# The memory's sum of squares behind the output projection, and memory values traced before a norm's element-wise part

## The chip, the core and the metric

One core of a Trainium2 chip runs the whole program in one launch. The metric is device time in microseconds. TensorE (PE) multiplies matrices and loads its weights (PEld) beside that; VectorE (DVE), ScalarE (ACT) and GpSimd (POOL) work element by element; SyncE (SP) issues most of the loads from memory. Each engine runs its own list of instructions in order, and waits on semaphores for the others.

## The reference

Two transformer blocks on 256 tokens of width 1024, everything in float32. The first: windowed and differential attention side by side, gated, merged, an output projection with a norm behind it, and a gated FFN (2816 wide), with a norm behind that. The second: a delta-rule mixer and a sparse latent attention, then cross-attention to a memory of 256 rows, then another FFN. What the change touches is the end of the first block and the memory's side of the cross-attention:

```python
# first block
merged = g_swa * (o_swa @ w_branch_swa[l]) + g_diff * (o_diff @ w_branch_diff[l])
h = h + rms_norm(merged @ w_out[l], post_mix_gain[l])
u = rms_norm(h, pre_ffn_gain[l])
...
# second block, cross-attention
mn = rmsnorm(mem, g_mem[l])
kvx = (mn @ w_xkv[l]).reshape(b, m_len, 2, X_HEADS, X_DH)
```

with `rmsnorm(x, g) = x * rsqrt(mean(x*x) + 1e-6) * g`. The memory does not depend on the tokens, so its keys and values can be computed at any time before the cross-attention.

## The kernel before

Tokens lie along the free axis: a tensor of 1024 features by 256 tokens is eight tiles of 128 x 256. A product is computed in halves for accuracy. ScalarE rounds a weight tile of 128 x 1024 to `wh` (L311; in a few places VectorE, L309), VectorE or GpSimd subtracts to get the rest `wl` (L313), and TensorE runs 24 matmuls for one output tile (`gemm`, L326): eight times `wh` with the activation's high and low half, then eight times `wl` with the high half. The raw tiles come by SyncE, three in flight; `wh` and `wl` have three buffers each.

The stages in question, in order:

- The branch projection `w_bs` (L813 to L823), eight groups. VectorE turns each result into a gated sum `mt` (L816, L817), ScalarE and VectorE split it into `m_h` and `m_l` (L287, L288). In the same loop `mem_split` (L776) works on the memory: VectorE makes its halves `mem_h` and `mem_l`, GpSimd squares its eight tiles and adds them up in `memt[:, 0]` (L781, L783).
- The memory's scale (L826 to L835): two matmuls with one column each (L388, one for 128 memory rows) sum the squares over the partitions; VectorE makes the rsqrt of the two columns by Newton steps (L377 to L381, L368 to L370), spreads it to two diagonals (L393), a matmul broadcasts it over the partitions (L833), and ScalarE copies that to `rsm` (L835). The result as a column, `rsm_t`, scales the memory's values.
- The output projection `w_out1` with `post_norm` (L837): eight groups; ScalarE keeps each result and its square, VectorE adds the squares (L401). Then the norm: a matmul with ones sums over the partitions (L351), `rsqrt_chain` (ScalarE's Ln and Exp, four steps on VectorE), eight products (L854) on VectorE, eight adds of the residual on GpSimd (L855), splits into `uh` and `ul` (L290, L291), squares again, and a second L351 with its rsqrt, whose scale is used only behind the FFN's products.
- `mem_keys` (L787): eight groups of the memory's keys; each result is multiplied by `rsm` on its way out of PSUM (L789).
- The first FFN, `ffn_in` (L871) and `w_fo1` with `post_norm` again (the norm before mixing), and behind it `mem_values` (L791), whose results are scaled by `rsm_t` (L806).

The order of the instructions on the engines is not the order of the code. A scheduler takes the program as traced, models its times, and builds each engine's list; a step traced earlier has precedence, and a tile of a pool has to be given back before the next with the same tag is used. The sums of both norms and of the memory and its broadcast are tiles `st` of the pool `ps_o`, tag `o`, one buffer:

```python
st = psum_pool.tile([P, 512], F32, name="st", tag="o")
pe.matmul(st[:, :n], ones, acc, start=True, stop=True)
```

So the order in which they are traced is the order in which they run.

Of the kernel before, what the change touches and what calls it, by code (L numbers as in the profile page):

```python
# [16 lines left out]
F32 = mybir.dt.float32  # L17
# [3 lines left out]
AF = mybir.ActivationFunctionType  # L21
# [4 lines left out]
P = 128  # L26
NT = 256
# [189 lines left out]
MEMG = 3  # L217
# [3 lines left out]
def _program(tc, d, out):  # L221
    nc = tc.nc
    ctx = ExitStack()
    pe, act, dve, pool, sp = nc.tensor, nc.scalar, nc.vector, nc.gpsimd, nc.sync
# [7 lines left out]
    with ctx:  # L232
# [12 lines left out]
        def carve(n, p=P):  # L245
            used[0] += n
            return base[:p, used[0] - n:used[0]]
# [8 lines left out]
        def G(n, j=0):  # L256
            o, w = _GC[n]
            return gcol[:, o + j:o + j + 1]
# [14 lines left out]
        ones_d = carve(P)  # L273
# [3 lines left out]
        ones_1 = carve(P)  # L277
# [70 lines left out]
        def rsqrt_of(psum_pool, acc, ones, n, out_t):  # L348

            st = psum_pool.tile([P, 512], F32, name="st", tag="o")  # L350
            pe.matmul(st[:, :n], ones, acc, start=True, stop=True)  # L351
            rsqrt_chain(st[:, :n], n, out_t)

        def rsqrt_chain(st, n, out_t, p=P):
            a = gpool.tile([P, NK], F32, name="rs_a", tag="rs_a", bufs=2)[:p, :n]
            b = gpool.tile([P, NK], F32, name="rs_b", tag="rs_b", bufs=1)[:p, :n]
            act.activation(a, st, AF.Ln, bias=eps[:p, :])
            act.activation(a, a, AF.Exp, scale=-0.5)
            dve.tensor_tensor(b, a, a, OP.mult)
            dve.scalar_tensor_tensor(b, st, EPS, b, OP.add, OP.mult)  # L360
            dve.tensor_scalar(b, b, -0.5, 1.5, OP.mult, OP.add)
            dve.tensor_tensor(out_t, b, a, OP.mult)

        def newton(y, h):

            t = gpool.tile([P, 16], F32, name="nt_t", tag="nt_t", bufs=2)[:, :y.shape[1]]
            for _ in range(3):
                dve.tensor_tensor(t, y, y, OP.mult)  # L368
                dve.tensor_tensor(t, t, h, OP.mult)
                dve.scalar_tensor_tensor(y, t, 1.5, y, OP.add, OP.mult)  # L370

        def rsqrt_tok(st, nb, add=EPS):

            m = gpool.tile([P, 16], F32, name="nt_m", tag="nt_m", bufs=2)[:, :nb]
            h = gpool.tile([P, 16], F32, name="nt_h", tag="nt_h", bufs=2)[:, :nb]
            y = gpool.tile([P, 16], F32, name="nt_y", tag="nt_y", bufs=2)[:, :nb]
            dve.tensor_scalar(m, st, add, None, OP.add)  # L377
            dve.tensor_scalar(h, st, -0.5, -0.5 * add, OP.mult, OP.add)
            yi = y.bitcast(I32)
            dve.tensor_scalar(yi, m.bitcast(I32), 1, None, OP.logical_shift_right)  # L380
            dve.tensor_scalar(yi, yi, -1.0, MAGIC, OP.mult, OP.add)  # L381
            newton(y, h)
            return y

        def sums_tok(dst, acc, col, nb):

            for b in range(nb):
                pe.matmul(dst[:, b:b + 1], acc[:, b * P:(b + 1) * P], col[:, 0:1], start=True, stop=True)  # L388

        def diag_tok(dg, y, nb, n):  # L390
            for b in range(nb):
                w = min(P, n - b * P)
                dve.tensor_scalar(dg[:, b * P:b * P + w], ident[:, :w], y[:, b:b + 1], None, OP.mult)  # L393
# [23 lines left out]
        opool = new_pool(b1, "ps_o", 1, PSUM)  # L417
# [5 lines left out]
        st = opool.tile([P, 512], F32, name="st", tag="o")  # L423
        for _ in range(WARM):
            tc.keep_in_program_order(pe.matmul(st[:, :P], one.to_broadcast([P, P]), one.to_broadcast([P, P]),
                                               start=True, stop=True))
# [10 lines left out]
        st = opool.tile([P, 512], F32, name="st", tag="o")  # L437
# [283 lines left out]
        qs, fill = [], list(range(16))  # L721
# [48 lines left out]
        mhp = new_pool(mhst, "memhl", side="right")  # L770
        mem_h = mhp.tile([P, 8, NT], F32R, name="mem_h")
        mem_l = mhp.tile([P, 8, NT], F32R, name="mem_l")
        memt = mhp.tile([P, KT, NT], F32, name="memt")
# [13 lines left out]
        def mem_keys():  # L787
            for j in range(8):
                gemm(d["w_xk"][j], mems, NT, lambda o, j=j: dve.tensor_tensor(kx[:, j, :], o, rsm, OP.mult))  # L789

        def mem_values(groups):  # L791
            for g in groups:
                ps = [mm.tile([P, 512], F32, name="mm", tag="mm") for _ in range(2)]
                for kh in range(2):
                    h, l = load_w(d["w_xv"][g][:, kh * 1024:(kh + 1) * 1024], KT)
                    for tb in range(2):
                        tok = slice(tb * P, (tb + 1) * P)
                        for k in range(4):
                            kk_ = 4 * kh + k
                            cols = slice(k * NT, (k + 1) * NT)  # L800
                            o = ps[tb][:, :NT]
                            pe.matmul(o, mem_h[:, kk_, tok], h[:, cols], start=(kk_ == 0), stop=False)
                            pe.matmul(o, mem_l[:, kk_, tok], h[:, cols], start=False, stop=False)
                            pe.matmul(o, mem_h[:, kk_, tok], l[:, cols], start=False, stop=(kk_ == 7))  # L804
                for tb in range(2):
                    dve.tensor_scalar(vx[:, tb, g * NT:(g + 1) * NT], ps[tb][:, :NT], rsm_t[:, tb:tb + 1], None,  # L806
                                      OP.mult)
# [15 lines left out]
            mem_split(j)  # L823

        tc.keep_in_program_order(act.preload_act_table_set(EXP_LN))
        st = opool.tile([P, 512], F32, name="st", tag="o")  # L826
        sums_tok(st, memt[:, 0, :], ones_d, 2)
        rsm_t = mhp.tile([P, 2], F32, name="rsm_t")
        dve.tensor_copy(rsm_t, rsqrt_tok(st[:, :2], 2))
        dg = mhp.tile([P, NT], F32, name="dgm")  # L830
        diag_tok(dg, rsm_t, 2, NT)
        st = opool.tile([P, 512], F32, name="st", tag="o")
        pe.matmul(st[:, :NT], ones_1, dg, start=True, stop=True)  # L833
        rsm = mhp.tile([P, NT], F32, name="rsm")
        act.activation(rsm, st[:, :NT], AF.Copy)  # L835

        def post_norm(src_w, xs, gain, res, res_out, g_next, whole=False):  # L837

            fg = mpool.tile([P, 8, NT], F32, name="fg", tag="fg")
            acc = gpool.tile([P, NK], F32, name="acc", tag="acc", bufs=1)[:, :NT]  # L840
            for j in range(8):
                def use(o, j=j):
                    act.activation(fg[:, j, :], o, AF.Copy, scale=G(gain, j))
                    sumsq(j, o, acc, NT)
                gemm_long(src_w[j], xs, NT, use)
            rr = gpool.tile([P, NK], F32, name="rs", tag="rs", bufs=2)
            rsqrt_of(opool, acc, ones_d, NT, rr[:, :NT])
            if whole:
                u = gpool.tile([P, KT, NK], F32, name="u", tag="uh")
            else:  # L850
                uh, ul = new_u()
            acc2 = gpool.tile([P, NK], F32, name="acc2", tag="acc2", bufs=1)[:, :NT]
            for j in range(8):
                dve.tensor_tensor(fg[:, j, :], fg[:, j, :], rr[:, :NT], OP.mult)  # L854
                pool.tensor_tensor(res_out[:, j, :], fg[:, j, :], res[:, j, :NT], OP.add)  # L855
                if whole:
                    act.activation(u[:, j, :NT], res_out[:, j, :], AF.Copy, scale=G(g_next, j))
                else:
                    split(uh[:, j, :NT], ul[:, j, :NT], res_out[:, j, :], G(g_next, j))
                sumsq(j, res_out[:, j, :], acc2, NT)  # L860
            rs2 = gpool.tile([P, NK], F32, name="rs", tag="rs", bufs=2)
            rsqrt_of(opool, acc2, ones_d, NT, rs2[:, :NT])
            if whole:
                return [u[:, k, :NT] for k in range(8)], rs2[:, :NT]
            return [(uh[:, k, :NT], ul[:, k, :NT]) for k in range(8)], rs2[:, :NT]

        h1 = rpool.tile([P, KT, NT], F32, name="h1", tag="resB")
# [3 lines left out]
        def ffn_in(pool_, src_w, us, rs, f_h, f_l):  # L871
            for j in range(FT):
# [7 lines left out]
                def use_u(o, sg=sg, j=j):  # L880
# [20 lines left out]
        relb = carve(8, 32)  # L901
        late(relb, d["rel_bias"])

        mem_keys()


# [16 lines left out]

        x1 = rpool.tile([P, KT, NK], F32, name="x1", tag="resA")[:, :, :NT]
        us, rs = post_norm(d["w_fo1"], [(f_h[:, k, :], f_l[:, k, :]) for k in range(FT)],
                           "post_ffn", h1, x1, "g_mix", whole=True)
        fst.close()


        mem_values(range(MEMG))  # L930

# [536 lines left out]
        for c in range(2):  # L1470
            gb = ppool.tile([P, 512], F32, name="s", tag="s")
            for h in range(4):
                pe.matmul(gb[:, h * P:(h + 1) * P], gg[:, 4 * c + h:4 * c + h + 1].to_broadcast([P, P]), triu,
                          start=True, stop=True)
# [88 lines left out]
        for h in range(4):  # L1563
# [28 lines left out]
            o = opool.tile([P, 512], F32, name="o", tag="o")  # L1592
            o = o.rearrange("p (a b) -> p a b", a=2)
# [105 lines left out]
```

## Time and profile before

| | |
|---|---|
| runs | 1011.46, 1011.47, 1014.0 us; median 1011.47 |
| the profiled execution | 1014.09 us, its span 1012.3 us |
| mean granted clock of TensorE | 0.984 of full speed |
| busy share of the span | TensorE 96%, weight loads 90%, VectorE 71%, ScalarE 54%, GpSimd 31% |
| branch projection | about 285 to 320 us |
| output projection | about 320 to 342 us |
| first norm and memory keys | about 342 to 380 us |
| norm before mixing, memory values | about 558 to 585 us |

The times of single instructions are counted from the start of the span. A row of the timeline merges equal instructions that follow each other: start, time from the first's start to the last's end, engine, line, what is written from what, and how many. Matmuls are pipelined, so a row's 0.28 us of one is longer than the 0.12 us from one start to the next. A releaser in brackets is what ended the engine's idle time just before.

### The profile page before, as it was taken

The numbers are of one execution on the slowest core, as the hardware profiler recorded it, in microseconds if no ns is written. First come the engines' busy times: TensorE is split into PE (matmuls) and PEld (weight loads), VectorE is DVE, ScalarE is ACT, GpSimd is POOL, SyncE is SP. The second block draws the span as 40 slices with busy tenths as digits, with TensorE's granted clock in tenths as the row PEclk, the third lists the DMA queues.
The fourth block names the chain that finished last, engine by engine and source line by source line (L and its number), as shares of the span: only waits on it lengthen the run. The fifth ranks groups of instructions, "written<-read, shape, count | busy, mean of one in ns | idle before, by whom it ended". The sixth has DMA issues, their size and how long they took to land. (4 is left out here: it accounts for less than half of the span.)

```text
span 1012.3 us, 18979 instructions
## 1 busy us (share of the span) xinstructions
PE 974.1 (96%) x7356; PEld 916.1 (90%) x7356; DVE 722.8 (71%) x1468; ACT 544.8 (54%) x1089; POOL 312.3 (31%) x294
## 2 busy tenths in 40 slices
PE   9889999999978999999999899999999999999996
PEld 8779999998978999999999788787799999999885
DVE  7998899887697696656455638977687676666444
ACT  4556677666544555555454444335666555555433
POOL 6865468655491032221100302221021002222002
PEclk9998999999997999999999899999999999999998
DMA  6333333333434555555666232333045255555552
GB/s 238 129 104 101 109 107 124 120 110 105 167 125 148 188 204 186 187 187 183 214 200 198 83 133 91 122 114 106 1 150 205 64 186 188 187 187 186 182 192 88
DMA packets 42026, 149.31 MB, mean 147 GB/s; under 512 B 4728, under 2 KB 5376, under 8 KB 41808
## 3 DMA queue, kind: packets, MB, share of 16 engines
q1 hardware_dynamic: 40896, 145.47, 42.6%
q0 software_dynamic: 608, 2.03, 0.7%
q8 instruction: 58, 0.95, 0.4%
q10 hardware_dynamic: 432, 0.59, 0.2%
q14 instruction: 32, 0.26, 0.1%
HBM read 147.01 MB, written 1.06 MB: 146 GB/s over the span
## 5 line engine op out<-in xcount | busy, mean ns | idle before, releaser
L311 ACT ACTIVATE wh<-raw 128x1024 fp32r<-128x1024 f32 (+1 forms) x244 | 256.2, 1052 | 222.7 <-PE mm L326 134.3
L313 DVE TENSOR_TENSOR wl<-raw,wh 128x1024 fp32r<-128x1024 f32 (+1 forms) x220 | 274.0, 1247 | 85.8 <-ACT wh L311 83.7
L326 PE MATMUL mm<-uh,wh 128*128 128x256 f32 (+1 forms) x1112 | 280.5, 287 | 1.3 <-DVE vbm L540 0.9
L326 PE MATMUL mm<-ul,wh 128*128 128x256 f32 (+1 forms) x1112 | 279.0, 286 | 0.2 <-DVE ul L291 0.2
L326 PEld LDWEIGHTS mm<-uh,wh 128*128 128x128 f32 x1112 | 211.1, 190 | 4.6 <-DVE vbm L540 1.1
L326 PEld LDWEIGHTS mm<-ul,wh 128*128 128x128 f32 x1112 | 211.5, 190 | 1.3 <-DVE ul L291 0.5
L326 PE MATMUL mm<-uh,wl 128*128 128x256 f32 (+1 forms) x1112 | 162.5, 285 | 0.0
L326 PEld LDWEIGHTS mm<-uh,wl 128*128 128x128 f32 x1112 | 145.2, 191 | 0.8 <-issue 0.3
L878 POOL TENSOR_TENSOR sg<-sg,rs 128x256 f32<-128x256 f32 x44 | 49.4, 1126 | 233.8 <-ACT sg L877 229.3
L313 POOL TENSOR_TENSOR wl<-raw,wh 128x1024 fp32r<-128x1024 f32 x30 | 72.4, 2414 | 51.9 <-ACT wh L311 51.9
L337 PE MATMUL mm<-u,raw 128*128 128x256 f32 x320 | 73.1, 382 | 0.2 <-DMA raw<-w_pr 0.2
L337 PEld LDWEIGHTS mm<-u,raw 128*128 128x128 f32 x320 | 59.5, 190 | 9.5 <-DVE y L995 0.6
L882 DVE TENSOR_TENSOR ft<-mm,sg 128x256 f32<-128x256 f32 x42 | 17.8, 424 | 52.0 <-PE mm L326 51.5
L326 PE MATMUL mm<-f_h,wh 128*128 128x256 f32 x176 | 41.1, 276 | 0.0
L326 PE MATMUL mm<-f_l,wh 128*128 128x256 f32 x176 | 41.1, 276 | 0.0
L876 DVE TENSOR_TENSOR sg<-mm,rs 128x256 f32<-128x256 f32 x40 | 17.0, 424 | 31.4 <-PE mm L326 31.3
L1633 PE MATMUL ac<-wh,f_h 128*128 128x512 f32 (+1 forms) x110 | 38.4, 349 | 0.0
L1636 PE MATMUL ac<-wh,f_l 128*128 128x512 f32 (+1 forms) x110 | 38.1, 347 | 0.0
L1637 PE MATMUL ac<-wl,f_h 128*128 128x512 f32 (+1 forms) x110 | 37.8, 347 | 0.0
L326 PEld LDWEIGHTS mm<-f_l,wh 128*128 128x128 f32 x176 | 33.0, 188 | 0.0
L326 PEld LDWEIGHTS mm<-f_h,wh 128*128 128x128 f32 x176 | 33.0, 188 | 0.0
L855 POOL TENSOR_TENSOR x<-fg,h 128x256 f32<-128x256 f32 x8 | 7.7, 997 | 66.6 <-PE mm L804 66.6
(544 smaller groups left out, 2205.8 us busy)
## 6 DMA issues: line engine op xcount, KB each, us to landing
raw<-w_gu SPq DMA_DIRECT2D x88, 512.0 KB, 4.3
raw<-w_dn SPq DMA_DIRECT2D x22, 512.0 KB, 3.7
raw<-w_pr SPq DMA_DIRECT2D x20, 512.0 KB, 3.6
raw<-w_gate SPq DMA_DIRECT2D x16, 512.0 KB, 3.6
raw<-w_out SPq DMA_DIRECT2D x16, 512.0 KB, 3.7
raw<-w_fo SPq DMA_DIRECT2D x16, 512.0 KB, 3.8
raw<-w_kb SPq DMA_DIRECT2D x8, 512.0 KB, 3.7
raw<-w_vb SPq DMA_DIRECT2D x8, 512.0 KB, 3.7
```

The lines of the kernel that those rows point to most:

```text
L311: act.activation(h[:, :kt * c], raw[:, :kt * c], AF.Copy)
L313: eng.tensor_tensor(l[:, :kt * c], raw[:, :kt * c], h[:, :kt * c].bitcast(F32), OP.subtract)
L326: pe.matmul(o, w[:, k * P:(k + 1) * P], xs[k][i], start=(first and n_ == 0), stop=(last and n_ == len(steps) - 1))
L337: pe.matmul(o, raw[:, k * P:(k + 1) * P], x, start=(k == 0), stop=(k == len(xs) - 1))
L855: pool.tensor_tensor(res_out[:, j, :], fg[:, j, :], res[:, j, :NT], OP.add)
L876: dve.tensor_tensor(sg, o, rs, OP.mult)
L878: pool.tensor_tensor(sg, sg, rs, OP.mult)
L882: dve.tensor_tensor(t, o, sg, OP.mult)
L1633: m = pe.matmul(o, f_h[:, k, tok], h[:, cols], start=(k == 0), stop=False)
L1636: pe.matmul(o, f_l[:, k, tok], h[:, cols], start=False, stop=False)
L1637: pe.matmul(o, f_h[:, k, tok], l[:, cols], start=False, stop=(k == FT - 1))
```

## The change

Two edits. The block that makes the memory's scale is traced behind the output projection's whole `post_norm`, just ahead of `mem_keys`, where it stood before the projection. And `post_norm` gets a parameter `fill`, a function that it calls between its first rsqrt and the element-wise part; the norm before mixing uses it to trace the first group of memory values there, and the other two follow behind it as before.

```diff
         tc.keep_in_program_order(act.preload_act_table_set(EXP_LN))
-        st = opool.tile([P, 512], F32, name="st", tag="o")
-        sums_tok(st, memt[:, 0, :], ones_d, 2)
-        rsm_t = mhp.tile([P, 2], F32, name="rsm_t")
-        dve.tensor_copy(rsm_t, rsqrt_tok(st[:, :2], 2))
-        dg = mhp.tile([P, NT], F32, name="dgm")
-        diag_tok(dg, rsm_t, 2, NT)
-        st = opool.tile([P, 512], F32, name="st", tag="o")
-        pe.matmul(st[:, :NT], ones_1, dg, start=True, stop=True)
-        rsm = mhp.tile([P, NT], F32, name="rsm")
-        act.activation(rsm, st[:, :NT], AF.Copy)
-
-        def post_norm(src_w, xs, gain, res, res_out, g_next, whole=False):
+        def post_norm(src_w, xs, gain, res, res_out, g_next, whole=False, fill=None):
...
             rsqrt_of(opool, acc, ones_d, NT, rr[:, :NT])
+            if fill is not None:
+                fill()
...
         late(relb, d["rel_bias"])
 
+        st = opool.tile([P, 512], F32, name="st", tag="o")
+        sums_tok(st, memt[:, 0, :], ones_d, 2)
...
+        rsm = mhp.tile([P, NT], F32, name="rsm")
+        act.activation(rsm, st[:, :NT], AF.Copy)
+
         mem_keys()
...
-                           "post_ffn", h1, x1, "g_mix", whole=True)
+                           "post_ffn", h1, x1, "g_mix", whole=True, fill=lambda: mem_values([0]))
         fst.close()
 
-        mem_values(range(MEMG))
+        mem_values(range(1, MEMG))
```

TensorE, in the branch projection; `os_h` and `os_l` are its activation halves, `memt` the squares of the memory. The row with a minus is the first of the two sums:

```order
 L326 MATMUL mm<-os_l,wh 128x256
 L326 MATMUL mm<-os_h,wl 128x256 x8
-L388 MATMUL st<-base,memt 128x1
 L326 MATMUL mm<-os_h,wh 128x256
 L326 MATMUL mm<-os_l,wh 128x256
```

What moved: the first sum stood between the fifth and the sixth group, the second (not shown) between the eighth and the first group of the output projection; both are gone from there.

TensorE, after the output projection, at the end of the second key group; `mem_h` and `mem_l` are the memory's halves, `acc` and `acc_4676` the sums of squares of the norm's first and second rsqrt:

```order
 L326 MATMUL mm<-mem_h,wh 128x256
 L351 MATMUL st<-acc,base 128x256
+L326 MATMUL mm<-mem_l,wh 128x256
+L326 MATMUL mm<-mem_h,wh 128x256
+L326 MATMUL mm<-mem_l,wh 128x256
+L326 MATMUL mm<-mem_h,wl 128x256 x8
+L351 MATMUL st<-acc_4676,base 128x256
+L388 MATMUL st<-base,memt 128x1 x2
+L902 MATMUL st<-dgm,base 128x256
+L326 MATMUL mm<-mem_h,wh 128x256
```

What moved: the second norm sum, the memory's two sums and its broadcast now stand right behind the second key group, and key groups 3 to 8 behind them. Before, the second norm sum stood inside the fourth FFN group.

VectorE, the same place, as it stands in the change (with the line numbers of the change; the other Newton steps and the copy to the column lie between the two pieces):

```order
L401 TENSOR_TENSOR acc_4676<-acc_4676,sq 128x256 x2
L1222 COPY small<-base 128x128
L1235 STREAM_SHUFFLE row<-small 128x16 x2
L359 TENSOR_TENSOR rs_b<-rs_a 128x256
L360 SCALAR_TENSOR_TENSOR rs_b<-st,rs_b 128x256
L361 TENSOR_SCALAR rs_b<-rs_b 128x256
L362 TENSOR_TENSOR rs<-rs_b,rs_a 128x256
L377 TENSOR_SCALAR nt_m<-st 128x2
...
L393 TENSOR_SCALAR dgm<-base,rsm_t 128x128 x2
L789 TENSOR_TENSOR kx<-mm,rsm 128x256 x3
```

What moved: the Newton steps stand behind the norm's last adds, a copy of a constant and the second rsqrt; they stood beside the end of the branch projection. The first three key evictions (L789) follow them in one piece; before, seven of the eight stood among the norm's steps. From the middle of the first FFN to the end of the program the lists of all engines are the same, but for the small matmul of the bias table (L916 before), which stood behind the fifth FFN group and now stands behind the last one, and the copy of its result.

## Rows read from the trace of the kernel before

**Rows 1.** Busy time, share of the span and instructions of each engine
```profile
PE 974.1 (96%) x7356; PEld 916.1 (90%) x7356; DVE 722.8 (71%) x1468; ACT 544.8 (54%) x1089; POOL 312.3 (31%) x294
```

**Rows 2.** What TensorE waited for, whole span: total us, times, longest
```profile
PE st L388 <- POOL memt L783: 7.9, 1, 7.9
PE mm L804 <- DVE wl L313: 5.0, 2, 4.4
```

**Rows 3.** TensorE in order of time: start, us, instruction, [idle before it <-releaser]
```profile
299.07 1.11 PE L326 MATMUL mm<-os_h,wl 128*128 128x256 f32 x8
...
308.07 0.59 PE L388 MATMUL st<-base,memt 128*128 128x1 f32 x2 [7.89 <-POOL memt L783]
```

**Rows 4.** Windows: length, busy of five engines, granted clock, DMA share, GB/s
```profile
303.00:304.00 1.00, 0.00 (x0) 0.00 (x0) 1.00 (x2) 0.00 (x0) 1.00 (x1) 0.82 0.00 0
...
313.00:314.00 1.00, 1.00 (x7) 1.00 (x7) 0.00 (x0) 0.73 (x2) 0.00 (x0) 0.56 0.00 0
314.00:315.00 1.00, 1.00 (x10) 1.00 (x10) 0.97 (x2) 0.00 (x0) 0.00 (x0) 1.00 0.00 0
```

**Rows 5.** VectorE in order of time, end of the branch projection
```profile
302.30 1.74 DVE L313 TENSOR_TENSOR wl<-raw,wh 128x1024 fp32r<-128x1024 f32 x1
...
310.03 0.41 DVE L288 TENSOR_TENSOR m_l<-mt,m_h 128x256 fp32r<-128x256 f32 x1
...
322.29 0.42 DVE L288 TENSOR_TENSOR m_l<-mt,m_h 128x256 fp32r<-128x256 f32 x1
```

**Rows 6.** Waits of all engines, 265 to 425 us
```profile
DVE mt L816 <- PE mm L326: 4.8, 3, 3.6
```

**Rows 7.** TensorE in order of time, output projection to first FFN groups
```profile
324.32 1.07 PE L326 MATMUL mm<-m_h,wl 128*128 128x256 f32 x8
...
346.42 0.59 PE L351 MATMUL st<-acc,base 128*128 128x256 f32 x2
...
347.20 1.12 PE L326 MATMUL mm<-mem_h,wl 128*128 128x256 f32 x8
...
373.20 0.28 PE L326 MATMUL s<-uh,wh 128*128 128x256 f32 x1
...
376.03 0.28 PE L326 MATMUL mm<-uh,wh 128*128 128x256 f32 x1
...
379.29 0.28 PE L326 MATMUL mm<-uh,wh 128*128 128x256 f32 x1
```

**Rows 8.** ScalarE in order of time, first rsqrt of the norm
```profile
347.05 0.47 ACT L357 ACTIVATE rs_a<-st,base 128x256 f32<-128x256 f32 x1 [1.90 <-PE st L351]
347.42 1.05 ACT L311 ACTIVATE wh<-raw 128x1024 fp32r<-128x1024 f32 x1
```

**Rows 9.** VectorE in order of time, the norm after the output projection
```profile
353.05 6.07 DVE L854 TENSOR_TENSOR fg<-fg,rs 128x256 f32<-128x256 f32 x8
...
360.73 1.35 DVE L291 SCALAR_TENSOR_TENSOR ul<-h,base,uh 128x256 fp32r<-128x256 f32 x2
...
363.81 1.26 DVE L291 SCALAR_TENSOR_TENSOR ul<-h,base,uh 128x256 fp32r<-128x256 f32 x3
...
378.51 0.42 DVE L359 TENSOR_TENSOR rs_b<-rs_a 128x256 f32<-128x256 f32 x1
```

**Rows 10.** GpSimd in order of time, the same norm
```profile
353.61 7.79 POOL L855 TENSOR_TENSOR h<-fg,hT 128x256 f32<-128x256 f32 x8 [45.60 <-DVE fg L854]
```

**Rows 11.** DMA issues, 260 to 400 us: count, KB, median us to landing
```profile
base<-const_b POOLq DMA_DIRECT2D x1, 384.0 KB, 5.7
```

**Rows 12.** VectorE in order of time, the memory's Newton steps
```profile
322.02 0.16 DVE L380 TENSOR_SCALAR nt_y<-nt_m 128x2 int32<-128x2 int32 x1
...
324.18 0.16 DVE L370 SCALAR_TENSOR_TENSOR nt_y<-nt_t,nt_y 128x2 f32<-128x2 f32 x1
```

**Rows 13.** TensorE in order of time, the norm before mixing
```profile
558.33 0.59 PE L351 MATMUL st<-acc,base 128*128 128x256 f32 x2
```

**Rows 14.** VectorE in order of time, the same norm
```profile
574.78 2.00 DVE L401 TENSOR_TENSOR acc<-acc,sq 128x256 f32<-128x256 f32 x4
```

More of the change, by code (lines that the diff above doesn't have):

```diff
@@ L902, in _program @@
         late(relb, d["rel_bias"])
+        st = opool.tile([P, 512], F32, name="st", tag="o")
+        sums_tok(st, memt[:, 0, :], ones_d, 2)
+        rsm_t = mhp.tile([P, 2], F32, name="rsm_t")
+        dve.tensor_copy(rsm_t, rsqrt_tok(st[:, :2], 2))
+        dg = mhp.tile([P, NT], F32, name="dgm")
+        diag_tok(dg, rsm_t, 2, NT)
+        st = opool.tile([P, 512], F32, name="st", tag="o")
+        pe.matmul(st[:, :NT], ones_1, dg, start=True, stop=True)
+        rsm = mhp.tile([P, NT], F32, name="rsm")
+        act.activation(rsm, st[:, :NT], AF.Copy)
         mem_keys()
```

## The prediction

> **What bounds the kernel now.** I read the busy line first: TensorE is busy 974.1 us of 1012.3, so 38 us of idle time are all that a reordering can win, and any new idle time there lengthens the run [rows 1]. Then the list of what TensorE waited for: the longest wait by far is 7.9 us, and it is the first of the two matmuls that this change moves, waiting for GpSimd's sum of squares of the memory [rows 2, 3]. [...] Last I read the engines in order of time through the branch projection, the output projection and the norm behind it, since there the order listing moves instructions.
>
> **Part 1: the wait that goes.** The wait ends at 308.07, and the matmuls then run at half clock until about 313.9, which costs half of 5.9 us, 2.9 us [rows 3, 4]. On paper 7.9 + 2.9 = 10.8 us come back. But VectorE runs without a gap up to the end of the fourth m_l subtraction (310.03 + 0.41 = 310.4), so nothing before that comes earlier [rows 5]. From there to the last m_l subtraction (ending 322.71) it spent 12.3 us, of which 4.8 were waits for the late TensorE [rows 5, 6], and 0.4 us were four small steps of the memory's rsqrt that now leave. So the last m_l is ready 5.2 us earlier, at 317.5. TensorE then has 18 matmuls of the first two output groups left, at 24 per 2.83 us (373.20 to 376.03) [rows 7]: done at 319.7. Before, the last eight of them started at 324.32 and took 0.95: 325.3 [rows 7]. I take a gain of 5.6 us. The ends are 10.8 (if VectorE's backlog hid nothing) and 2.7 (if the thin stretch around 312 to 317 us, where TensorE now waits piecemeal for m_h and m_l, brings the clock down once more, another 2.9).
>
> **Part 2: the wait that comes.** In the new order the memory's two sums and the broadcast of its scale stand behind the second key group *and* behind the norm's second sum (the L351 on the second accumulator). All these borrow one small PSUM pool, and the listing puts them in one file: norm sum, memory sums, broadcast, then key groups 3 to 8. Before, key groups 2 to 8 and the first FFN groups ran beside the norm's element-wise work. Now TensorE stands still from the end of key group 2 until the whole chain is through. Behind the waiting matmul are six key groups (17 us of work at 2.83) and all of the FFN; on ScalarE six weight casts stand behind the copy of the scale; on VectorE the key evictions stand behind the Newton steps. Key group 2 ends at 347.20 + 0.95 = 348.2 before, so at 342.6 now [rows 7]. From there, step by step:
> - VectorE still subtracts one weight tile, whose cast ends at 347.42 + 1.05 - 5.6 = 342.9 [rows 8]; with 1.2 us for it, 344.1.
> - The four steps of the first rsqrt at 0.42 each [rows 9]: 345.8.
> - The eight products, slowed by GpSimd's adds beside them, 6.07 us [rows 9]: 351.9.
> - Eight ul subtractions and seven adds of squares. Three run while GpSimd still adds, at 0.68; the others at about 0.4 [rows 9, 10]: between 6.3 and 7.0 us, I take 6.6: 358.5.
> - Norm sum to ScalarE's Ln 0.63 (346.42 to 347.05) [rows 7, 8], Ln and Exp 0.9: 360.0. VectorE also has a copy of a constant before its next step, which GpSimd's queue fetches only after its adds: 345.8 + 0.56 + 7.79 + 5.7 for the landing = 359.9 [rows 10, 11], then 0.4 for three small steps: 360.3. The two arrive together.
> - Two rsqrt steps, after which the bank is free, 0.85; the two memory sums about 0.6: 361.7.
> - Newton: 322.02 to 324.34 before, less one subtraction between (0.42), is 1.9 [rows 12]; two first steps, the copy and the two diagonals about 0.85 more: 364.5.
> - Broadcast and ScalarE's copy, again 0.63 + 0.4: 365.5; with the three small matmuls at half clock, 366.0.
>
> So TensorE idles 23.4 us, and key group 3 starts at 366.0 instead of 348.2: 17.8 us later, the 5.6 already taken off. As a check, the norm ahead of the mixing block has the same chain with memory values beside it: its first sum is at 558.33, its last add of squares ends at 576.8, 18.4 us [rows 13, 14]; mine is 340.8 to 358.5, 17.7 us.
>
> After so long an idle stretch the clock is at half, and I charge the 2.9 us of the stop at 300 to 314 us [rows 4]. Something comes back: between key group 3 and the end of the fourth FFN group TensorE needed 31.1 us (348.2 to 379.29) for ten groups that take 28.3 at 2.83, and 0.2 for the norm's sum; the remaining 2.6 us were waits for pieces of the norm that are long done now [rows 7]. Three key groups have their weights cast before the stop, so the casts behind the copy come in time, and SyncE's loads, three tiles ahead, wait with them at no cost.
>
> **Part 3: edits with no price.** The first memory values are traced ahead of the element-wise part of the norm before mixing. In the listing nothing moves there: TensorE, VectorE and ScalarE have the same order before and after, because the scheduler had put these values beside that norm already. The 4.4 us wait of that place, the greater part of the second row of [rows 2], therefore stays: 0 us. The matmul that makes the bias table moves behind the first FFN's last group: one small matmul at another place, and its two DMAs keep their place in GpSimd's queue behind the FFN's products: 0 us.
>
> **The sum.** +17.8 + 2.9 - 2.6 = +18.1 us. The profiled execution took 1014.1 us (span 1012.3), 2.6 above the median of the runs, 1011.5. Its sum is 1032.2; on the median it is 1029.6, and I predict **1030 us**. TensorE is the bound in all later stages, so nothing there takes the delay up.
>
> **The rivals.**
> - *The clock falls a second time* (0.14). In the thin stretch of part 1 TensorE has about 3.4 us of matmuls in 6.8 us. For it: the earlier fall came in a stretch of standing still. Against it: each of these gaps is under 2 us, where that fall came some 3 us into one unbroken wait [rows 4]. Price 2.9: 1033.
> - *A shorter chain* (0.14). Without weight subtractions and key evictions between them, VectorE's products and GpSimd's adds may run closer. At 0.42 a product the eight take 3.4 instead of 6.07, if GpSimd's 7.79 shrinks as well, and the constant lands earlier; two more us from the small steps. Price -5: 1025. Against it: the 6.07 and the 7.79 are of eight products and eight adds that ran back to back already [rows 9, 10].
> - *The queue does not hold* (0.02), the case on the other side. If matmuls of key groups 3 to 8 could pass the waiting sums, only part 1 would remain: 1011.5 - 5.6 = 1006. It decides from the point where a ready matmul starts before an older one that waits. Against it: at 304.04 the last weights of the next branch group were ready, and TensorE stood until 308.07 behind the one waiting sum [rows 3, 5], with no weight load either [rows 4].
>
> [...]
>
> - *The gaps cancel* (0.05). To come out even, key group 3 would have to start by 347.9, a gap of 5.3 us. GpSimd's adds alone take 7.79 [rows 10], so this needs the built order to matter less than listed, by some cover that I do not see.
>
> **How the numbers follow.** Forecast 0.65 (1026 to 1035), second fall of the clock 0.14, shorter chain 0.14, cancelling 0.05, passing 0.02. A difference under 0.3% (3 us) can't be told from none here. All but the last two are slower by more than that: slower 0.93; cancelling is spread over same and faster, 0.03 and 0.02; with passing, faster 0.04. The range takes in the second fall of the clock and most of the shorter chain: 1023 to 1036.
>
> **What would show it.** In the changed profile: no wait of TensorE for the memory's sums near 300 us and a full clock there; one gap of 20 to 24 us after the second key group, released by VectorE and ScalarE in three pieces (norm sum, memory sums, broadcast); half clock for some 6 us behind it; then no waits until the fourth FFN group. A wait of 4 to 5 us for memory values in the next norm, as before. I am wrong if that gap is under 10 us, if key matmuls run beside the norm's products, or if the branch projection still waits as long.

## The result and the profile after

The changed kernel took 1030.57 us (median of 4 runs, 1030.2 to 1031.01) against 1012.08 us of the kernel before (4 runs, 1011.46 to 1014.0): the ratio is 1.0181, with a 95% interval of 1.0169 to 1.0193. It is slower by 18.5 us, and the 1030 us that were predicted came true to 0.6. The profiled execution took 1030.91 us, with a span of 1029.1. That is 16.8 above the profiled execution before, and not 18.5: in the norm before mixing, where the engines have the same order in both kernels, the clock fell in both executions, but in the changed kernel's for a shorter time. Nearly the same work, first before, then after, as windows (length, busy time and instructions of PE, PEld, DVE, ACT, POOL, granted clock, DMA share, GB/s):

```profile
560.00:585.00 25.00, 20.59 (x128) 19.58 (x128) 17.23 (x31) 9.83 (x21) 7.71 (x8) 0.86 0.26 85
```

```profile
578.70:604.00 25.30, 20.89 (x135) 19.75 (x134) 17.37 (x31) 10.32 (x24) 7.70 (x8) 0.93 0.25 84
```

The comparison of the kernels therefore rests on the medians, and that of their stages on rows ahead of this norm.

TensorE's list of waits, whole span (total us, times, longest):

```profile
PE st L351 <- DVE acc L401: 15.7, 1, 15.7
PE mm L804 <- DVE wl L313: 5.0, 2, 4.4
PE st L902 <- DVE dgm L393: 3.2, 1, 3.2
...
PE mm L326 <- DVE m_l L288: 2.2, 2, 1.6
...
PE st L388 <- issue: 2.0, 1, 2.0
```

The 7.9 us wait for the memory's squares [rows 2] is gone. At the head stands a wait that the kernel before did not have: the norm's second sum waits 15.7 us for the last add of squares. The memory's sums (L388) and the broadcast (L902) follow with 2.0 and 3.2. The row for the memory values (L804) is unchanged.

TensorE in order of time (start, us, instruction, idle before it and releaser), branch projection first, then the norm's first sum and the gap:

```profile
312.43 0.39 PE L326 MATMUL mm<-m_l,wh 128*128 128x256 f32 x1 [0.57 <-DVE m_l L288]
314.57 0.39 PE L326 MATMUL mm<-m_l,wh 128*128 128x256 f32 x1 [1.64 <-DVE m_l L288]
...
340.90 0.59 PE L351 MATMUL st<-acc,base 128*128 128x256 f32 x2
...
341.69 1.12 PE L326 MATMUL mm<-mem_h,wl 128*128 128x256 f32 x8
358.48 1.22 PE L351 MATMUL st<-acc,base 128*128 128x256 f32 x2 [15.68 <-DVE acc L401]
361.68 0.99 PE L388 MATMUL st<-base,memt 128*128 128x1 f32 x4 [1.98 <-issue]
365.90 1.19 PE L902 MATMUL st<-dgm,base 128*128 128x256 f32 x2 [3.23 <-DVE dgm L393]
367.57 0.58 PE L326 MATMUL mm<-mem_h,wh 128*128 128x256 f32 x1 [0.47 <-ACT rsm L904]
...
374.26 1.12 PE L326 MATMUL mm<-mem_h,wl 128*128 128x256 f32 x8
```

This is the trade in a few rows. At the branch projection two short waits for `m_l` are left. Key group 2 ends at 342.6, 5.5 us earlier than before [rows 7], and key group 3 starts at 367.57: a gap of 24.9 us in which TensorE runs the norm's second sum, the memory's two sums and the broadcast.

The same stretch by windows:

```profile
311.00:316.00 5.00, 2.79 (x22) 2.40 (x21) 5.00 (x10) 2.19 (x4) 0.00 (x0) 1.00 0.75 256
...
346.00:350.00 4.00, 0.00 (x0) 0.00 (x0) 4.00 (x7) 2.64 (x7) 3.61 (x5) 0.72 0.18 74
350.00:360.00 10.00, 1.22 (x2) 0.50 (x2) 8.72 (x23) 4.13 (x11) 6.00 (x9) 0.50 0.30 98
360.00:368.00 8.00, 2.61 (x8) 1.87 (x9) 4.65 (x22) 1.01 (x3) 0.00 (x0) 0.50 0.01 2
368.00:372.00 4.00, 4.00 (x22) 4.00 (x22) 0.30 (x1) 0.61 (x1) 0.00 (x0) 0.54 0.00 0
372.00:380.00 8.00, 8.00 (x69) 8.00 (x68) 4.67 (x6) 2.56 (x3) 0.00 (x0) 1.00 0.39 131
```

The granted clock stays at full (1.00 in the windows from 300 to 322 us) through the branch projection, where it had fallen before [rows 4], to 0.50 from 304 to 313 us. By the means of the windows it falls to half (0.50) at about 347.8, 5 us into the gap, and is back at full at about 371.7. In the ten microseconds from 350 VectorE is busy for 8.72: TensorE is waiting for it.

VectorE and GpSimd in the gap, the rows that answer to [rows 9, 10]:

```profile
345.82 5.96 DVE L845 TENSOR_TENSOR fg<-fg,rs 128x256 f32<-128x256 f32 x8
...
357.49 0.94 DVE L401 TENSOR_TENSOR acc<-acc,sq 128x256 f32<-128x256 f32 x2
...
360.69 0.42 DVE L359 TENSOR_TENSOR rs_b<-rs_a 128x256 f32<-128x256 f32 x1 [1.83 <-ACT rs_a L358]
...
362.70 0.16 DVE L377 TENSOR_SCALAR nt_m<-st 128x2 f32<-128x2 f32 x1 [0.34 <-PE st L388]
```

```profile
346.39 6.83 POOL L846 TENSOR_TENSOR h<-fg,hT 128x256 f32<-128x256 f32 x8 [38.57 <-DVE fg L845]
```

The eight products take what they took before (5.96 against 6.07 us), GpSimd's adds 1 us less. The norm as a whole got shorter: from its first sum to its last add of squares it takes 17.5 us (340.90 to 358.43), where the kernel before needed 27.8 (346.42 [rows 7] to the end of this row of VectorE):

```profile
373.77 0.42 DVE L401 TENSOR_TENSOR acc<-acc,sq 128x256 f32<-128x256 f32 x1
```

There, eight weight subtractions and seven key evictions stood between its steps, and TensorE worked beside them. What is new is that TensorE stands still beside the norm.

### The profile page after: what moved, and what is told of

Read it like the earlier page. It is cut to its first block, busy times and chain, and to the rows that moved or that the text cites. A ratio compares the mean times of both kernels' runs of the same rounds, so it can differ in the third digit from the quotient of the medians.

```text
span 1029.1 us, 18986 instructions
## 1 busy us (share of the span) xinstructions
PE 975.5 (95%) x7356; PEld 916.1 (89%) x7356; DVE 722.4 (70%) x1468; ACT 546.4 (53%) x1089; POOL 312.0 (30%) x294
## 5 line engine op out<-in xcount | busy, mean ns | idle before, releaser
L873 DVE TENSOR_TENSOR ft<-mm,sg 128x256 f32<-128x256 f32 x42 | 17.8, 424 | 54.2 <-PE mm L326 54.0
```

What stands on the lines that cost most here:

```text
L873: dve.tensor_tensor(t, o, sg, OP.mult)
```

## The experiments

Ratios are to the kernel before on the same chip, whose median there was between 1012.1 and 1013.8 us, so kernels of different chips are compared by their ratios. A ratio is formed from all runs and can differ by 0.1% from that of the medians.

**Each half alone.** `e1_move_only` takes the `fill` out of the changed kernel:

```diff
-"post_ffn", h1, x1, "g_mix", whole=True, fill=lambda: mem_values([0]))
+"post_ffn", h1, x1, "g_mix", whole=True)
...
-mem_values(range(1, MEMG))
+mem_values(range(MEMG))
```

> Only the first half of the change: the memory's sums and scale move behind the output projection, the first memory values stay where they were. Theory (the fill moves nothing): the time of the whole change, 1030.5 us, within 2 us. Rival (the values ahead of the element-wise part take something back or cost something): more than 3 us away from 1030.5, in either direction.

Measured: 1031.3 us, ratio 1.0178 (1.0159 to 1.0197), that of the whole change. `e2_fill_only` is the reverse, the kernel before with only the `fill`.

> Only the second half of the change: the first memory values are traced ahead of the element-wise part of the norm before mixing, the memory's scale stays where it was. Theory: the scheduler had these values beside that norm already, so the time is that of the kernel before, 1011 to 1013 us, and TensorE's wait of 4.4 us for the values' weights stays. Rival (the values now begin earlier): up to 4.4 us less, some 1008 us.

Measured: 1013.16 us, ratio 1.0001 (0.9990 to 1.0011). Its list of waits begins with the same two rows as [rows 2]: 7.9 us for the squares, 4.4 us the longest for the values. So the theory held. The whole effect is the move of the scale.

**What holds the sums back.** `e5_pool` leaves the block where the change puts it and gives its two PSUM tiles another pool:

```diff
-st = opool.tile([P, 512], F32, name="st", tag="o")
+st = tpool.tile([P, 512], F32, name="t", tag="t")
```

> The changed kernel, but the memory's sums and broadcast take their PSUM tiles from a free two-buffer pool instead of the one-buffer pool that they share with the norm's two sums. Theory (it is the one buffer of that pool that holds the sums behind the norm's second sum): with another pool the sums are issued early again, as in the kernel before, with its 7.9 us wait for GpSimd's squares, and the time is that of before, 1011 to 1013 us. Rival (the place in the program sets the order, whatever the pool): 1030.5 us as the changed kernel.

Measured: 1013.36 us, ratio 0.9999 (0.9988 to 1.0010), and in TensorE's order of time the old wait is back:

```profile
307.53 0.59 PE L388 MATMUL t<-base,memt 128*128 128x1 f32 x2 [7.89 <-POOL memt L783]
```

So the place in the program alone does nothing. The buffer that the sums share with the norm does it all: it keeps them behind the norm's second sum, and with buffers of their own the scheduler puts them back where they were.

**What holds the keys back.** `e7_noscale` copies the keys out of PSUM without the scale, so that their two PSUM buffers come free without it:

```diff
-gemm(d["w_xk"][j], mems, NT, lambda o, j=j: dve.tensor_tensor(kx[:, j, :], o, rsm, OP.mult))
+gemm(d["w_xk"][j], mems, NT, lambda o, j=j: dve.tensor_copy(kx[:, j, :], o))
```

> The changed kernel with the memory keys copied out unscaled: the kernel leaves out the multiplication of the keys by the memory's scale (the scale is still computed). Theory (the whole loss is the keys and the FFN standing behind the scale): the gap behind key group 2 goes, only the gain of the branch projection stays, some 1006 us, 5.6 under the kernel before. Rival (the gap comes from the norm's own chain or from the small sums' place on TensorE): 1022 to 1030.5 us.

Measured: 1007.21 us, ratio 0.9940 (0.9917 to 0.9963), 5 to 6 us less than before; L351, L388 and L902 do not stand in its list of waits at all. In TensorE's list the sums are no longer ahead of the key groups. The third key group's last matmuls, the norm's second sum and the memory's sums:

```profile
344.70 1.12 PE L326 MATMUL mm<-mem_h,wl 128*128 128x256 f32 x8
...
371.00 0.59 PE L351 MATMUL st<-acc,base 128*128 128x256 f32 x2
...
375.92 0.50 PE L388 MATMUL st<-base,memt 128*128 128x1 f32 x4
```

The scale's chain is still there and costs nothing, since no key waits for its result: the loss came from six key groups, and the FFN in the queue behind them, having no PSUM to go to until the scale was there.

`e6_banks` keeps the scale and gives key groups 3 to 5 three other banks, unused at that time:

```diff
+ps = ppool.tile([P, 512], F32, name="s", tag="s") if 2 <= j < 5 else None
-gemm(d["w_xk"][j], mems, NT, lambda o, j=j: dve.tensor_tensor(kx[:, j, :], o, rsm, OP.mult))
+gemm(d["w_xk"][j], mems, NT, lambda o, j=j: dve.tensor_tensor(kx[:, j, :], o, rsm, OP.mult), ps=ps)
```

> The changed kernel, but key groups 3 to 5 write to three free banks of the attention's score pool instead of the two-buffer pool of the key groups 1 and 2, so they need not wait for an eviction that needs the memory's scale. Theory (the gap is expensive because buffers that wait for the scale keep the keys behind the chain): three groups of 2.83 us go into the gap and TensorE stays warm longer, 8.5 us less than the changed kernel, some 1022 us (1020 if the half clock behind the gap shrinks too). Rival (the scale's chain holds the keys by the order of TensorE alone, whatever the buffers): 1030.5 us, no change.

Measured: 1025.74 us, ratio 1.0126 (1.0107 to 1.0146), 5.6 us less than `e1_move_only` on the same chip. The three groups do run in the gap, and TensorE's longest wait falls to 10.7 us. But 8.5 us were expected. VectorE in order of time shows where the rest went, with the TensorE row that it releases:

```profile
351.19 1.74 DVE L313 TENSOR_TENSOR wl<-raw,wh 128x1024 fp32r<-128x1024 f32 x1
...
353.71 1.21 DVE L313 TENSOR_TENSOR wl<-raw,wh 128x1024 fp32r<-128x1024 f32 x1
...
357.11 1.21 DVE L313 TENSOR_TENSOR wl<-raw,wh 128x1024 fp32r<-128x1024 f32 x1
...
360.47 1.48 DVE L401 TENSOR_TENSOR acc<-acc,sq 128x256 f32<-128x256 f32 x3
```

```profile
362.01 1.22 PE L351 MATMUL st<-acc,base 128*128 128x256 f32 x2 [10.74 <-DVE acc L401]
```

The running key groups free weight buffers, so the next weights are split, and three subtractions (4.2 us) stand in the middle of the chain that TensorE waits for. The last add of squares ends at 361.95, 3.5 us later than in the changed kernel (358.43): 8.5 less 3.5 is 5.0, near the 5.6 that were measured.

**What the clock costs.** `e9_keepclock` fills the gap of the changed kernel with matmuls whose results nobody uses (a constant times an old tile of the memory's squares). `issue_after` holds an instruction behind another one; the 38 matmuls ahead of the norm's second sum come from a call that the cut leaves out:

```diff
+def warm(n):
+    warm_t = tpool.tile([P, 512], F32, name="t", tag="t")
+    with tc.issue_after(last_rs[0].ins):
+        for _ in range(n):
+            last_rs[0] = pe.matmul(warm_t[:, :NT], ones_1, memt[:, 1, :], start=True, stop=True)
...
+warm(4)
 st = opool.tile([P, 512], F32, name="st", tag="o")
 sums_tok(st, memt[:, 0, :], ones_d, 2)
+warm(6)
```

> The changed kernel with 48 added matmuls on constants (results unused): 38 between the norm's two sums, 4 between the norm's second sum and the memory's sums, 6 between these and the broadcast, to keep TensorE running in the gap at an unchanged chain of waits. Theory (half clock costs 1.6 us in the small sums and 2.0 us in the first groups behind the gap): 3.6 us less than the changed kernel, some 1027 us, with a granted clock of 1.00 from 340 to 372 us. Rival (the loss is the chain on VectorE alone and the clock costs nothing on the path): 1030.5 us, or more by what the added matmuls delay.

Measured: 1029.08 us, ratio 1.0156 (1.0141 to 1.0171), 2.5 us less than the changed kernel by the ratios, though the two intervals touch. From 340 us on the windows are at full clock:

```profile
340.00:358.00 18.00, 18.00 (x88) 15.94 (x87) 15.22 (x33) 7.43 (x18) 9.64 (x13) 1.00 0.32 100
358.00:368.00 10.00, 8.06 (x47) 6.82 (x46) 6.10 (x23) 2.34 (x4) 0.00 (x0) 1.00 0.16 53
368.00:372.00 4.00, 4.00 (x36) 4.00 (x35) 1.56 (x2) 1.12 (x2) 0.00 (x0) 1.00 0.01 4
```

In the profiles the first FFN output group starts 2.5 us earlier than in the changed kernel (510.01 against 512.53). Of that, 1.8 come from the groups behind the gap and only 0.7 from the sums: key group 3 starts at 366.85 instead of 367.57. The lags of the sums did shrink. From the norm's second sum to ScalarE's Ln it is 0.63 us here, where the changed kernel has 1.26:

```profile
357.57 0.59 PE L362 MATMUL st<-acc,base 128*128 128x256 f32 x2
```

```profile
358.20 0.47 ACT L370 ACTIVATE rs_a<-st,base 128x256 f32<-128x256 f32 x1 [5.59 <-PE st L362]
```

From the broadcast to its copy it is 0.71 for 1.23, and the two sums take 0.50 for 0.99. But the chain of waits did not stay as it was: part of key group 2 now lies between the added matmuls, and a weight subtraction stands ahead of the Newton steps, where the changed kernel has one ahead of the first rsqrt (342.99 us):

```profile
361.37 1.23 DVE L313 TENSOR_TENSOR wl<-raw,wh 128x1024 fp32r<-128x1024 f32 x1 [0.54 <-ACT wh L311]
362.52 0.15 DVE L390 TENSOR_SCALAR nt_m<-st 128x2 f32<-128x2 f32 x1
```

So keeping the clock gave back about a seventh of the loss in this run; its share in an unchanged chain is not shown. Most of the loss is the waits on VectorE.

**The wait without the chain.** `e3_hold2` starts from the kernel before. It calls the same block inside the output projection, behind the third group, and holds the two sums behind that group's last matmul:

```diff
+def mem_scale():
+    st = opool.tile([P, 512], F32, name="st", tag="o")
+    with tc.issue_after(last_mm[0].ins):
+        sums_tok(st, memt[:, 0, :], ones_d, 2)
...
                 gemm_long(src_w[j], xs, NT, use)
+                if mid is not None and j == 2:
+                    mid()
```

> The memory's two sums are held behind the third group of the output projection, and the scale's broadcast comes a few groups later in the same projection; all else is in the order of the kernel before. So the wait for the memory's squares goes and the chain behind key group 2 does not come. Theory (VectorE's unbroken run up to 310 us hides half of the wait): 5.6 us less than the kernel before, some 1006 us. Rival (all 10.8 us of wait and half clock come back): some 1001 us. Second rival (the wait was hidden anyway and only the chain counts): no change, 1011.5 us.

Measured: 1010.02 us (10 runs, 1008.6 to 1011.71), ratio 0.9974 (0.9964 to 0.9985). That is faster by some 2.5 us and none of the three expectations: half of the 5.6 us is missing. Two windows of the profile show where, first `e3_hold2`:

```profile
311.00:314.00 3.00, 0.91 (x6) 0.51 (x4) 3.00 (x8) 1.52 (x3) 0.00 (x0) 1.00 0.76 266
314.00:318.00 4.00, 3.88 (x19) 3.89 (x20) 2.62 (x6) 1.96 (x3) 0.00 (x0) 0.57 0.78 234
...
362.00:366.00 4.00, 4.00 (x24) 4.00 (x23) 4.00 (x8) 0.00 (x0) 0.00 (x0) 0.57 0.93 320
```

and the changed kernel:

```profile
314.00:318.00 4.00, 3.28 (x25) 3.05 (x26) 3.08 (x7) 2.26 (x4) 0.00 (x0) 1.00 0.70 232
```

The two kernels have the same waits for `m_l` here, 0.57 and 1.64 us in both. In `e3_hold2` the clock fell to half behind them, in the changed kernel it did not. A mean of 0.57 over 4 us is a loss of 1.7. Of that, some 1.0 is left at the end of the first two output groups: from the second wait's end it is 6.0 us there (314.12 to 320.1) and 4.9 in the changed kernel (314.57 to 319.5). The clock fell once more beside the first FFN groups, behind waits of 1.0 and 0.2 us for pieces of the norm: 1.7 again. 5.6 less 1.0 and 1.7 is 2.9; the spans differ by 2.8. The kernel before has the same two waits of 1.0 and 0.2 us there and kept the full clock. Of the profiled kernels with these two waits for `m_l`, four show the fall behind them (`e3_hold2`, `e6_banks`, `e7_noscale`, `e9_keepclock`) and two do not (the changed kernel, `e1_move_only`). Of the eight with the waits of 1.0 and 0.2 us, three show a fall there (`e3_hold2`, 0.57 in the row above, `e8_castb`, and `e11_hold_wl`, 0.62 and 0.53 over 2 us each). Whether the clock falls a second time, the prediction's first rival, is thus not settled by these waits, and differs between executions.

**The thin stretch.** `e8_castb` gives three weight casts of the branch projection from VectorE to ScalarE, on top of `e3_hold2`:

```diff
-hshare[0] = 1 if j in (0,1,2,3,4,5) else 0
+hshare[0] = 1 if j in (0,1,2) else 0
```

> The kernel with the memory's sums held behind the third output group (e3_hold2), and the weight casts of branch groups 4 to 6 on ScalarE instead of VectorE: three casts of some 1.2 us less on VectorE, which ran without a gap up to the last m_l subtraction. Theory (VectorE's backlog is what eats the rest of the 10.8 us): the last m_l comes up to 3.5 us earlier, TensorE's two waits of 0.6 and 1.6 us for m_l go, and the half clock behind them with them: 3 to 4 us less than e3_hold2, some 1006 us. Rival (another resource than VectorE, the weights' arrival or ScalarE, sets the pace there): 1010 us, as e3_hold2, or more if ScalarE's casts come late.

Measured: 1010.84 us, ratio 0.9973 (0.9961 to 0.9984), no gain over `e3_hold2`. TensorE does end the branch projection 1.6 us earlier (308.81 against 310.39), but the waits of 0.8 and 1.6 us for `m_l` stay, and the profiled execution has half clock behind them too. By the first FFN output group 1.4 us of lead are left in the profile; the runs, which lie 1008.0 to 1013.1 for this kernel, don't resolve it.

The theory of `e8_castb` thus missed. What stands between the `m_l` pieces is weight subtractions for later output groups. `e11_hold_wl` holds those behind the last `m_l`, and `e10_hold_wl` adds the casts of `e8_castb`:

```diff
+hold_l[0] = last_l[0] if mid is not None and j in (1, 2, 3) else None
 gemm_long(src_w[j], xs, NT, use)
+hold_l[0] = None
...
+with tc.issue_after(hold_l[0].ins):
+    eng.tensor_tensor(l[:, :kt * c], raw[:, :kt * c], h[:, :kt * c].bitcast(F32), OP.subtract)
```

> The kernel with the memory's sums held behind the third output group (e3_hold2), and the weight subtractions of output groups 2 to 4 on VectorE held behind the last m_l subtraction; nothing else moves. Theory (the stretch around 312 us is thin because two of these subtractions, 1.2 us each, stand between the m_l pieces on VectorE): the last m_l comes 2.4 us earlier, TensorE's two waits of 0.6 and 1.6 us go, and with them the half clock that the profiles of three of these kernels showed behind them (1.8 us): 2 to 4 us less than e3_hold2, 1006 to 1008 us. Rival (the time of these kernels scatters with the clock elsewhere and this stretch is not what limits): 1010 us, as e3_hold2.

> As e11_hold_wl, with the weight casts of branch groups 4 to 6 on ScalarE as in e8_castb. Theory: TensorE's branch projection ends 1.5 us earlier, as the profile of e8_castb showed, and now nothing in the thin stretch gives it back: 1 to 2 us less than e11_hold_wl, 1005 to 1006 us, the fastest of these kernels. Rival (what VectorE gains here is lost again behind, as in e8_castb): no difference to e11_hold_wl.

Measured: `e11_hold_wl` 1009.19 us, ratio 0.9960 (0.9945 to 0.9974); `e10_hold_wl` 1009.54 us, ratio 0.9953 (0.9935 to 0.9972). These are the fastest kernels here with the whole computation, 4 to 5 us under the kernel before. Both miss what was expected, 1006 to 1008 and 1005 to 1006 us. Against each other and against `e3_hold2` the intervals overlap, so the step from one to the next is not shown by the times. In the profiles the waits for `m_l` get shorter and do not go: 0.52 and 0.69 us in `e11_hold_wl`, 0.78 and 0.70 in `e10_hold_wl`. Counted from the first output matmul, the last `m_l` of `e11_hold_wl` is ready 1.3 us earlier than in `e3_hold2` (5.2 against 6.5 us), not 2.4, since it now waits 0.48 us for ScalarE's `m_h`. In `e10_hold_wl` the windows are at full clock:

```profile
310.00:312.00 2.00, 0.66 (x3) 0.46 (x4) 1.75 (x6) 0.83 (x2) 0.00 (x0) 1.00 0.58 166
312.00:318.00 6.00, 5.93 (x49) 5.72 (x50) 5.32 (x8) 5.29 (x8) 0.00 (x0) 1.00 0.38 125
```

Its seven runs lie from 1005.54 to 1011.96 us, a spread larger than the difference between these kernels. Where the longer ones lose their time stays open, since one execution of each kernel was profiled; that of `e11_hold_wl` was at full clock around 312 us, but fell to half beside the first FFN groups (0.62 and 0.53 in the windows from 360 to 364 us).

## Why the prediction was right

**Part 1 held.** The last `m_l` was ready at 317.2 (317.5 was predicted), TensorE was through the first two output groups at 319.5 (319.7), and key group 2 ended at 342.6 (342.6). That VectorE's backlog ate part of the rest of the 10.8 us shows where work is taken out of its way: the keys start at 342.0 before, at 336.5 in the changed kernel, at 337.8 in `e3_hold2` (some 1.0 of it half clock) and at 334.3 in `e10_hold_wl`, 7.7 us earlier than before. The times put the worth of this part at some 2.5 us (`e3_hold2`) and 5 to 6 (`e7_noscale`), for the 5.6 that were taken.

**Part 2 held step by step, until the clock.** In us, the changed kernel:

| end of the step | predicted | profile after |
|---|---|---|
| last weight subtraction | 344.1 | 344.2 |
| first rsqrt | 345.8 | 345.8 |
| eight products | 351.9 | 351.8 |
| adds of squares | 358.5 | 358.4 |
| Ln and Exp | 360.0 | 360.7 |
| memory sums | 361.7 | 362.7 |
| Newton steps, diagonals | 364.5 | 365.7 |
| key group 3 starts | 366.0 | 367.6 |

Up to the adds of squares VectorE sets the pace, and all is within 0.1 us. What is 1.6 us late at the end is for the greater part half clock, a term that was mis-sized: the small matmuls were given 0.5 us for it. From the start of the norm's sum to ScalarE's Ln it was 0.63 us in [rows 7, 8], and it is 1.26 now:

```profile
359.74 0.47 ACT L357 ACTIVATE rs_a<-st,base 128x256 f32<-128x256 f32 x1 [5.36 <-PE st L351]
```

The same lag stands once more behind the broadcast (365.90 to the copy at 367.13), and the two sums took 0.99 us where 0.6 was taken: half clock cost 1.6 us in all, 1.1 more than the 0.5 of the forecast. At full clock, in `e9_keepclock`, the three take 0.63, 0.71 and 0.50. The other 0.5 of the delay are the Newton steps and diagonals (3.05 us where 2.75 was taken) and hand-overs of some 0.1 between the engines, which the forecast left out. A second term was too large. The groups behind the gap lost 1.9 us to the clock, not 2.9: the last eight matmuls of key group 4 begin at 374.26, where 372.37 would be their time at full clock (367.57 and 40 matmuls of 0.12). Key group 3 is 19.4 us later than before (348.2), and with 1.9 that is 21.3. At the first matmul of the FFN's output groups the profiles differ by 18.7 (493.82 before, 512.53 after), so 2.6 us came back, as much as the waits that the forecast named:

```profile
493.82 0.28 PE L326 MATMUL mm<-f_h,wh 128*128 128x256 f32 x1
```

```profile
512.53 0.39 PE L326 MATMUL mm<-f_h,wh 128*128 128x256 f32 x1
```

The forecast had +17.8, +2.9 and -2.6, the profiles +19.4, +1.9 and -2.6: two errors of opposite sign, both mostly of the clock, nearly cancel. That the median came within 0.6 us is in part luck; that the loss came from the chain is not. The gap itself is 24.9 us, just above the 20 to 24 that were named as a sign, and half clock lasted some 4 us behind it, not 6.

**One step of the chain was wrong and cost nothing.** The constant was to arrive with ScalarE's Exp; it landed after 3.4 us instead of 5.7 [rows 11], and VectorE copied it at 358.34, 2 us ahead of need.

**The reason for the order was half of the reason.** The prediction named the small PSUM pool that makes the file of sums, and `e5_pool` shows that this is what decides. It took for granted that key groups 3 to 8 must stand behind it. `e7_noscale` and `e6_banks` show why they did: the keys' two buffers wait for the scale as well, and where they don't, the key groups stand ahead of the sums.

**Part 3 held**: nothing moves and nothing is won (`e2_fill_only`).

**The rivals.** The shorter chain is refuted by the table, and the second fall of the clock did not come in this kernel's profile. Passing was not put to the test behind key group 2, since the key groups there had no buffer either; this the prediction had overlooked. It was put to the test once more in `e5_pool`: the next branch group's weights were ready at 303.5, its PSUM buffer, by the order of the evictions, at 303.8, and its first matmul started at 307.98, behind the waiting sum. Neither here nor in the kernel before [rows 3] did a matmul start in the 7.89 us in which TensorE stood before that sum.

## What to carry to other kernels

A step is not cheap because it is small: ask which buffers its result sets free, and what is queued behind their next use. Before a step is moved later, look for a shared one-buffer pool that will tie it to a longer chain, and for results that can't leave PSUM without it; the better move here was to hold two tiny matmuls behind three output groups (`e3_hold2`, 1010.02 us), not behind a whole norm (1030.57 us). When such a wait goes, read what limited the engines inside it: of the 10.8 us here key group 2 ended only 5.5 us earlier, because VectorE's backlog held the rest, and waits of 0.57 and 1.64 us for `m_l` stood in its place.

## What the runs showed of the hardware

The order of the instructions and these waits do not settle the granted clock: behind the same two waits (0.5 to 0.6 and 1.64 us) it fell to half in four profiled executions (means of 0.57 over 4 us in `e3_hold2` and `e9_keepclock`) and stayed full in two (1.00 in the changed kernel). Behind a long stop it did not fall at a fixed time either: 3.5 us after TensorE stopped in the kernel before [rows 3, 4], and in the gap behind key group 2 after 5.1 us in the changed kernel (342.6 to 347.8), but after 2.6 us in `e1_move_only` (342.8 to 345.4), which has the same gap. Runs of one kernel can differ by 3 to 6 us (1008.6 to 1011.71 in ten runs of `e3_hold2`, 1005.54 to 1011.96 in seven of `e10_hold_wl`), so a microsecond can be read in a profile but hardly in the times.
